# A gated residual block on one core: branch B's third stream as block products, weight sums added by transfers, and several steps reordered

## The chip, the cores and the metric

The kernel runs on one core of one Trainium2 chip. TensorE (PE in the profile) multiplies, VectorE (DVE), ScalarE (ACT) and GpSimd (POOL) do the rest, SyncE (SP) issues most transfers. The metric is the device time of one execution in microseconds (us).

## The reference

One trunk layer on 512 positions of 1024 channels, all float32. Cut to what matters here:

```python
h = rmsnorm(x, norm_mix_g)
u, v, bg, cg, xs, ga, gb = jnp.split(h @ w_in, ..., axis=-1)
a = spatial_gating(gelu(u), rmsnorm(gelu(v), norm_v_g), w_s, b_s)
c = bg * causal_dwconv(cg * xs, conv_w)
m = sigmoid(ga + b1) * (a @ w_proj_a) + sigmoid(gb + b2) * (c @ w_proj_b)
x = x + m @ w_out
z = relu(rmsnorm(x, norm_ff_g) @ w_ff1)
y = rmsnorm(x + (z * z) @ w_ff2, norm_final_g)
```

Branch B has three streams: `cg`, `xs` and `bg`, each a product of `h` with a 1024 x 1024 matrix.

## The kernel before

Everything is held transposed: channels on the 128 partitions, the 512 positions along the free dimension. Each float32 operand is split into a rounded high part (`whi`, by ScalarE, L117) and a low rest (`wlo`, by VectorE, L118), and each product is three matmuls: high x high, high x low, low x high.

Two kinds of product exist. A **unit** makes one tile of 128 output channels by 8 k-steps x 3 = 24 matmuls of 512 columns (`unit_k`, L265 to L267). A **pair** makes two tiles at once by Strassen's method in Winograd's form: seven products P1, P2, E, P6, F, P7, D, each of 4 k-steps x 3 = 12 matmuls of 256 columns (L283 to L285), 84 in all. For that the weights need sums: `s31` (two blocks, one addition of 128x1024, L218) and `s42` (two additions of 128x512, L222 and L223), so a pair splits 3.5 operands of 128x1024 where two units split 2. P1, P6, P7 and D accumulate in one half bank of PSUM, called A; E and F in another, E; P2 stands alone. Between products ScalarE copies A and E out (L300, L305, L308, L314) and VectorE adds (L301, L309, L315). P7 and D of a pair run late, inside whatever products come next (`run_late`).

Pairs are used for both gates (4 pairs each), for `cg` and `xs` (4 each) and for the first feed-forward matrix (16); units for u, `bg`, both projections, w_out and the second feed-forward matrix. Weights arrive by SyncE transfers of 1 MB into two buffers `raw`, and a list of steps (load, split, sum) is worked off a step at a time between products (`pump`), with four buffers for split operands.

The stages in order: v (0 to 51 us; 16 k-steps of 12 matmuls, bound to x and w_v coming in; its root of the mean square `rstd_of` is taken at its middle), u and mixing, gate A with projection A (to 194), four times `c_pair` (a pair for `cg`, a pair for `xs`, two units for `bg`, conv on VectorE; to 330), gate B with projection B, w_out (to 441), and four chunks of the feed-forward part (5, 4, 4 and 3 pairs, each chunk followed by units). In the first of these pairs the second `rstd_of` is taken, spread over the partitions and copied to `Rf`, which every z needs. A scheduler puts the instructions in the order in which it thinks them ready, so the order on an engine differs from the code's.

Of the kernel before, what the change touches and what calls it, by code (L numbers as in the profile page):

```python
# [36 lines left out]
def hybrid_block(ctx, tc, xT, vecs, w_v, w_main, w_pair, w_s, b_s, out_a, out_b):  # L37
# [100 lines left out]
    def load(n):  # L138
# [8 lines left out]
        else:  # L147
            nc.sync.dma_start(r, w_pair[i])
# [56 lines left out]
    sums_t = None  # L205

    def plan_pair():
# [6 lines left out]
        s31, s42 = sums_t[0].t, sums_t[1].t  # L214

        def add1():

            nc.vector.tensor_tensor(s31, raw(1, 3), raw(3, 4).broadcast_to([P, 2, S]), op=ALU.add)  # L218

        def add2():  # L220

            nc.vector.tensor_tensor(s42[:, 1, :], s31[:, 1, :], raw(1, 2)[:, 0, :], op=ALU.add)  # L222
            nc.vector.tensor_tensor(s42[:, 0, :], s42[:, 1, :], raw(0, 1)[:, 0, :], op=ALU.add)  # L223
# [3 lines left out]
        add_step(add1)  # L227
        tl["s31"] = add_operand(lambda: s31)
        add_step(add2)
        tl["s42"] = add_operand(lambda: s42)  # L230
# [58 lines left out]
    def block_pair(p, right, first, second):  # L289
# [17 lines left out]
        product(p, right, "F", E, False)  # L307
        nc.scalar.copy(c1[:, N2:], A)  # L308
# [73 lines left out]
    sums_t = slots(2, "wsum")  # L382
# [4 lines left out]
    for _ in range(KS):  # L387
        plan_pair()
        plan_pair()
        plan_units(2)  # L390
# [25 lines left out]
    def prep_v(i):  # L416
# [11 lines left out]
        nc.sync.dma_start(t, w_v[h, k])  # L428
        if i == KT + 1 or i == KT + 4:
# [6 lines left out]
        if h == 0:  # L436
            sum_squares(acc, xin[k], k)
# [27 lines left out]
    for i in range(2 * KT):  # L465
# [4 lines left out]
        if i == KT - 1:  # L470
            r = rstd_of(acc)
        vp = vparts.pop(i)
# [8 lines left out]
        if i == KT - 1:  # L481
            for b in range(NB):
                v_gelu(0, b)
        if KT <= i < KT + NB:
            v_sq(0, i - KT)
# [95 lines left out]
    for p in range(KS):  # L581
        gate(next_pair(), 0, 2 * p, sgs.__setitem__)
        if p == 0:
            for g in range(KT - LAG, KT):
                mix(g)
            give(*vt_s, *ws_s)
            ah, al = hi_lo(a_s)
# [14 lines left out]
    def c_pair(j0):  # L602
# [201 lines left out]
    wait_rf = []  # L804

    def ff1_pair(p):
# [10 lines left out]
        if p == 0:  # L817
            r2 = rstd_of(acc)
# [93 lines left out]
```

## Time and profile before

| | |
|---|---|
| time, median of 3 runs | 796.01 us (795.35 to 796.61) |
| profiled execution: time | 796.82 us |
| profiled execution: span | 795.0 us |
| TensorE busy | 786.3 us (99%) |
| VectorE busy | 567.1 us (71%) |
| ScalarE busy | 362.6 us (46%) |
| GpSimd busy | 6.3 us (1%) |
| mean granted TensorE clock | 0.996 of 2.4 GHz |

The ends of matmuls are modelled and overlap, so TensorE's 99% says that it seldom stood still, and the distance between the starts of two matmuls says how fast it went. The DMA share is the mean busy share of the core's 16 DMA engines.

### The profile page before, as it was taken

Reading aid. Unit: us, or ns where it says so; the run is one execution under the profiler, and the core shown is the slowest. Engines: PE = TensorE matmul, PEld = TensorE weight load, DVE = VectorE, ACT = ScalarE, POOL = GpSimd, SP = SyncE. Lnnn points to the kernel's source line nnn. Section 1 sums busy time; section 2 is a strip of 40 time slices with the busy share of each in tenths; the row PEclk is TensorE's granted clock in tenths of the full one; section 3 lists DMA queues with packets and bytes.
Section 4 is the critical chain, followed back from the end, with each engine's and each line's share of the span. In section 5 each row is a group of like instructions: output and inputs, shape, how many; then the busy total and the mean of one; then the engine's idle time right before and its main releaser. Section 6 shows DMA issues by size and latency. Waiting matters only on the chain.

```text
span 795.0 us, 11578 instructions
## 1 busy us (share of the span) xinstructions
PE 786.3 (99%) x4798; PEld 703.6 (88%) x4798; DVE 567.1 (71%) x854; ACT 362.6 (46%) x548; POOL 6.3 (1%) x14
## 2 busy tenths in 40 slices
PE   9999999999999999999999999999999999999996
PEld 6888899899899998988888999889988998889886
DVE  7848785556989889766679888556855687557644
ACT  8525354343344443434455566324742365226421
POOL 0000000000000000000000000000000000000000
PEclk9999999999999999999999999999999999999999
DMA  9602113321332323333633023430353025311403
GB/s 343 226 15 97 62 55 106 106 106 54 109 120 92 106 84 129 106 107 106 212 106 106 1 106 109 157 106 1 106 179 140 1 87 178 106 54 54 159 1 106
DMA packets 21444, 83.61 MB, mean 105 GB/s; under 512 B 1936, under 2 KB 2960, under 8 KB 17296
## 3 DMA queue, kind: packets, MB, share of 16 engines
q1 hardware_dynamic: 20384, 81.27, 29.3%
q10 hardware_dynamic: 1008, 1.61, 0.6%
q8 instruction: 37, 0.61, 0.3%
q14 instruction: 15, 0.12, 0.0%
HBM read 80.78 MB, written 2.10 MB: 104 GB/s over the span
## 4 chain that ended last, share of the span: by engine, by line
PE 90%; DVE 4%; DMA 3%; ACT 1%; issue 1%; POOLq 0%; DVEq 0%; ACTq 0%
PE bank L266 16%; PE bank L265 16%; PE bank L267 16%; PE bank L283 12%; PE bank L285 11%; PE bank L284 11%; PE bank L476 6%; DVE wlo L118 2%; DMA raw<-w_pair 1%; DMA raw<-w_main 1%; ACT whi L117 1%; PE bank L530 1%; DMA vec<-vecs 0%; DVE z L118 0%; DVE wsum L218 0%
## 5 line engine op out<-in xcount | busy, mean ns | idle before, releaser
L117 ACT CAST whi<-raw 128x1024 fp32r<-128x1024 f32 (+1 forms) x136 | 128.8, 950 | 185.0 <-PE bank L266 122.8
L118 DVE TENSOR_TENSOR wlo<-raw,whi 128x1024 fp32r<-128x1024 f32 (+1 forms) x136 | 148.6, 1095 | 16.7 <-ACT whi L117 14.9
L266 PE MATMUL bank<-z,whi 128*128 128x512 f32 (+1 forms) x272 | 102.7, 377 | 0.4 <-DVE z L118 0.4
L265 PE MATMUL bank<-z,whi 128*128 128x512 f32 (+1 forms) x272 | 102.8, 378 | 0.0
L267 PE MATMUL bank<-z,wlo 128*128 128x512 f32 (+1 forms) x272 | 102.4, 377 | 0.0
L117 ACT CAST whi<-wsum 128x1024 fp32r<-128x1024 f32 x64 | 67.2, 1050 | 77.0 <-PE bank L266 41.2
L118 DVE TENSOR_TENSOR wlo<-wsum,whi 128x1024 fp32r<-128x1024 f32 x64 | 78.2, 1221 | 26.6 <-ACT whi L117 26.2
L283 PE MATMUL bank<-ft,whi 128*128 128x256 f32 x256 | 73.7, 288 | 0.2
L283 PE MATMUL bank<-xc,whi 128*128 128x256 f32 x256 | 73.2, 286 | 0.2
L284 PE MATMUL bank<-ft,whi 128*128 128x256 f32 x256 | 73.0, 285 | 0.0
L285 PE MATMUL bank<-ft,wlo 128*128 128x256 f32 x256 | 72.5, 285 | 0.0
L285 PE MATMUL bank<-xc,wlo 128*128 128x256 f32 x256 | 72.4, 283 | 0.0
L284 PE MATMUL bank<-xc,whi 128*128 128x256 f32 x256 | 72.4, 283 | 0.0
L837 DVE TENSOR_TENSOR res<-bank,res 128x512 f32<-128x512 f32 x30 | 20.7, 691 | 65.5 <-PE bank L267 65.5
L266 PEld LDWEIGHTS bank<-z,whi 128*128 128x128 f32 x272 | 51.2, 188 | 9.7 <-DVE z L118 0.7
L267 PEld LDWEIGHTS bank<-z,wlo 128*128 128x128 f32 x272 | 51.2, 188 | 9.4
L265 PEld LDWEIGHTS bank<-z,whi 128*128 128x128 f32 x272 | 51.2, 188 | 9.3 <-ACT z L117 0.3
L283 PE MATMUL bank<-fb,whi 128*128 128x256 f32 x192 | 54.9, 286 | 0.0
L283 PE MATMUL bank<-x,whi 128*128 128x256 f32 x192 | 54.5, 284 | 0.0
L284 PE MATMUL bank<-fb,whi 128*128 128x256 f32 x192 | 54.4, 284 | 0.0
L285 PE MATMUL bank<-fb,wlo 128*128 128x256 f32 x192 | 54.3, 284 | 0.0
L284 PE MATMUL bank<-x,whi 128*128 128x256 f32 x192 | 54.3, 283 | 0.0
(157 smaller groups left out, 1799.6 us busy)
## 6 DMA issues: line engine op xcount, KB each, us to landing
raw<-w_main SPq DMA_DIRECT2D x36, 1024.0 KB, 5.0
raw<-w_pair SPq DMA_DIRECT2D x32, 1024.0 KB, 4.8
vraw<-w_v SPq DMA_DIRECT2D x16, 256.0 KB, 5.4
xin<-xT SPq DMA_DIRECT2D x8, 256.0 KB, 5.2
res<-xT SPq DMA_DIRECT2D x8, 256.0 KB, 4.6
out_a<-o SPq DMA_DIRECT2D x4, 256.0 KB, 2.4
wsT<-w_sT ACTq DMA_DIRECT2D x2, 256.0 KB, 4.6
bsb<-b_sb ACTq DMA_DIRECT2D x2, 256.0 KB, 5.0
```

The costliest lines, as they stand in the source:

```text
L117: nc.scalar.copy(hi, src)
L118: nc.vector.tensor_tensor(lo, src, hi.bitcast(F32), op=ALU.subtract)
L265: nc.tensor.matmul(psum, hi[:, c], act_hi[k][:, cols], start=k == 0, stop=False)
L266: nc.tensor.matmul(psum, hi[:, c], act_lo[k][:, cols], start=False, stop=False)
L267: nc.tensor.matmul(psum, lo[:, c], act_hi[k][:, cols], start=False, stop=k == KT - 1)
L283: nc.tensor.matmul(out, w_hi, x_hi, start=first and sl == 0, stop=False, skip_group_check=True)
L284: nc.tensor.matmul(out, w_hi, x_lo, start=False, stop=False, skip_group_check=True)
L285: nc.tensor.matmul(out, w_lo, x_hi, start=False, stop=sl == KS - 1, skip_group_check=True)
L476: nc.tensor.matmul(vbanks[h][b], xs[k][:, b * P : (b + 1) * P], ws, start=k == 0 and ws is vh and xs is xh, stop=k == KT - 1 and xs is xl,)
L530: nc.tensor.matmul(pm[:, b * P : (b + 1) * P], vt[b][g // 4][:, (g % 4) * P : (g % 4 + 1) * P], wsT[:, g, :], start=True, stop=True,)
L837: nc.vector.tensor_add(res[j], py, res[j])
```

## The change

Four edits:

1. `bg` becomes a third pair in each `c_pair`: its weights move from the list of units to `w_pair` (36 pairs instead of 32), and the products with `y` are taken in `b_first` and `b_second`.
2. `s31` is made by transfers: GpSimd issues a copy of two weight blocks into a buffer and a second transfer that adds the third block to both (`accum_op`). One buffer at first, three after gate A's first pair. VectorE's addition of L218 goes; `raw` gets three of the four blocks.
3. In a pair, P1, P2 and E/F have a half bank each in three banks (before: two), and the copies out of A and E stand right behind their products.
4. Steps move: v's sums of squares four k-steps later, its root from behind step 6 to behind step 7 of the first half; the copy to `Rf` behind P7 of the first feed-forward pair; in the last chunk P7 and D are no longer flushed ahead of the units, and the first two units run side by side, with their last two k-steps at the end.

```diff
-            nc.sync.dma_start(r, w_pair[i])
+            nc.sync.dma_start(r[:, :3, :], w_pair[i, :, :3, :])
...
+    s31_free, s31_of, built = [], {}, [0]
+    def build():
+        while s31_free and built[0] < w_pair.shape[0]:
+            i, s = built[0], s31_free.pop(0)
+            built[0] += 1
+            s31_of[i] = s
+            nc.gpsimd.dma_start(s.t, w_pair[i, :, 1:3, :])
+            nc.gpsimd.dma_start(s.t, w_pair[i, :, 3:4, :].broadcast_to([P, 2, S]), accum_op=ALU.add)
...
-        def add1():
-            nc.vector.tensor_tensor(s31, raw(1, 3), raw(3, 4).broadcast_to([P, 2, S]), op=ALU.add)
+        def done1():
+            s31_free.append(s31_of.pop(n))
+            build()
...
-        ba, be = bank(), bank()
-        A, P2, E = ba[:, :N2], ba[:, N2:], be[:, :N2]
+        A, P2, E = (bank()[:, :N2] for _ in range(3))
         c1, c2 = temp("c1"), temp("c2")
         product(p, right, "P1", A, True)
-        product(p, right, "P2", P2, False)
         nc.scalar.copy(c1[:, :N2], A)
+        product(p, right, "P2", P2, True)
         nc.vector.tensor_add(c1[:, :N2], P2, c1[:, :N2])
         run_late()
         product(p, right, "E", E, True)
+        nc.scalar.copy(c2[:, N2:], E)
         product(p, right, "P6", A, False)
-        nc.scalar.copy(c2[:, N2:], E)
+        nc.scalar.copy(c1[:, N2:], A)
         run_late()
         product(p, right, "F", E, False)
-        nc.scalar.copy(c1[:, N2:], A)
         nc.vector.tensor_add(c1[:, N2:], E, c1[:, N2:])
...
-        if h == 0:
-            sum_squares(acc, xin[k], k)
+        if KS <= i < KS + KT:
+            sum_squares(acc, xin[i - KS], i - KS)
...
-        if i == KT - 1:
+        if i == KT:
             r = rstd_of(acc)
+            for b in range(NB):
+                v_gelu(0, b)
...
-        pbs = []
-        for e in range(2):
-            pbs.append(bank())
-            unit_matmuls(pbs[e], xh, xl)
-        for e in range(2):
-            nc.vector.tensor_mul(ys[e], pbs[e], ys[e])
-            split_into(ch[j0 + e], cl[j0 + e], ys[e])
+        def b_first(c1):
+            nc.vector.tensor_mul(c1, c1, ys[0])
+            split_into(ch[j0], cl[j0], c1)
+        def b_second(n21, c2):
+            y = ys[1]
+            for h, src in ((0, n21), (1, c2[:, N2:])):
+                cs = slice(h * N2, (h + 1) * N2)
+                nc.vector.scalar_tensor_tensor(c2[:, cs], src, -1.0, y[:, cs], op0=ALU.mult, op1=ALU.mult)
+            split_into(ch[j0 + 1], cl[j0 + 1], c2)
+        block_pair(next_pair(), right_x, b_first, b_second)
...
-        if ck == NCH - 1:
-            flush_late()
...
+        pys = side_by_side(zh, zl) if last else {}
```

The order on the engines shows three places. GpSimd, from its last memset at the start of the program to its first power for a root (`r`; `wsum` is the buffer of `s31`), before:

```order
L71 MEMSET inv_d 128x1
L73 MEMSET expo 128x4
L352 TENSOR_TENSOR r_316<-ms_314,expo 128x4 [waits DVE_49,Pool_49]
L352 TENSOR_TENSOR r_546<-ms_544,expo 128x4 [waits DVE_49,Activation_49,Pool_49]
L352 TENSOR_TENSOR r_4197<-ms_4195,expo 128x4 [waits DVE_49,Pool_49]
```

and of the change:

```order
L71 MEMSET inv_d 128x1
L73 MEMSET expo 128x4
L213 DMA wsum_104<-w_pair 128x1024
L214 DMA wsum_104<-w_pair 128x2x512 [waits DMASW0_49]
L362 TENSOR_TENSOR r_336<-ms_334,expo 128x4 [waits DVE_49,Pool_49]
L362 TENSOR_TENSOR r_548<-ms_546,expo 128x4 [waits DVE_49,Activation_49,Pool_49]
```

The first pair's two transfers now stand at the very start, with no wait ahead of the first. Next TensorE in gate A's second pair, before, where F begins (`x4`) and P6 (`xc20`) is put in between; bank 1133 holds A and P2, bank 1134 E and F:

```order
L283 MATMUL bank_1134<-x4_113,whi_1099 128x256 [waits Activation_49]
L284 MATMUL bank_1134<-x4_113,whi_1099 128x256
L285 MATMUL bank_1134<-x4_113,wlo_1100 128x256
L283 MATMUL bank_1134<-x5_114,whi_1099 128x256
L284 MATMUL bank_1134<-x5_114,whi_1099 128x256
L283 MATMUL bank_1133<-xc20_442,whi_1099 128x256 [waits DVE_49]
L284 MATMUL bank_1133<-xc20_442,whi_1099 128x256
```

and of the change, where P6 follows E (`xc13` is E's last k-step):

```order
L294 MATMUL bank_1142<-xc13_648,whi_1074 128x256
L295 MATMUL bank_1142<-xc13_648,whi_1074 128x256
L296 MATMUL bank_1142<-xc13_648,wlo_1075 128x256
L294 MATMUL bank_1140<-xc20_444,whi_1122 128x256 [waits Activation_49]
L295 MATMUL bank_1140<-xc20_444,whi_1122 128x256
L296 MATMUL bank_1140<-xc20_444,wlo_1123 128x256 [waits DVE_49]
```

P6's first matmul waited for VectorE (the addition that reads P2 in A's bank) and now waits for ScalarE (the copy of A). Last VectorE at the end of a `c_pair`, before (`y` times the units' banks, the split of c):

```order
L218 TENSOR_TENSOR wsum_103<-raw 128x1024
L645 TENSOR_TENSOR y<-bank,y 128x512
L118 TENSOR_TENSOR wlo<-raw,whi 128x1024
L118 TENSOR_TENSOR c_1688<-y,c_1688 128x512
L301 TENSOR_TENSOR c_2321<-bank,c_2321 128x256
```

and of the change:

```order
L663 SCALAR_TENSOR_TENSOR c_1913<-bank,y 128x256
L118 TENSOR_TENSOR wlo<-raw,whi 128x512
L319 TENSOR_TENSOR c_2042<-bank,c_2042 128x256
L118 TENSOR_TENSOR c_1699<-c_1913,c_1699 128x512
```

The addition of 128x1024 is gone from VectorE, and the product with `y` is done by halves, with the pair's own additions between.

## Rows read from the trace of the kernel before

**Rows 1.** The page's first part: busy us, share of the span, instructions.
```profile
PE 786.3 (99%) x4798; PEld 703.6 (88%) x4798; DVE 567.1 (71%) x854; ACT 362.6 (46%) x548; POOL 6.3 (1%) x14
```

**Rows 2.** Timeline of PE in gate A: start us, duration us, engine, line.
```profile
112.43 0.28 PE L283 MATMUL bank<-xc,whi 128*128 128x256 f32 x1
112.54 0.28 PE L284 MATMUL bank<-xc,whi 128*128 128x256 f32 x1
...
113.86 0.40 PE L265 MATMUL bank<-a,whi 128*128 128x512 f32 x1
114.09 0.40 PE L266 MATMUL bank<-a,whi 128*128 128x512 f32 x1
```

**Rows 3.** Chain that ended last: start us, duration us, what.
```profile
5.58 19.88 PE bank L476 x84
...
205.43 0.23 PE bank L266
...
236.56 0.23 PE bank L266
```

**Rows 4.** Waits of PE's weight loads: us in total, times, longest.
```profile
PEld bank L283 <- DVE c L301: 2.8, 10, 0.6
...
PEld bank L283 <- ACT c L305: 1.4, 7, 0.2
...
PEld bank L266 <- DVE z L118: 0.7, 1, 0.7
PEld st L359 <- DVE acc L379: 0.6, 1, 0.6
```

**Rows 5.** Timeline of gate A's second pair, all engines.
```profile
128.75 0.42 DVE L301 TENSOR_TENSOR c<-bank,c 128x256 f32<-128x256 f32 x1
...
129.22 0.39 PE L283 MATMUL bank<-xc,whi 128*128 128x256 f32 x1
```

**Rows 6.** Chain at the start of the feed-forward part.
```profile
444.72 0.60 DVE acc L379
...
446.53 0.35 DVE c L301
```

**Rows 7.** Windows: from:to, length, busy us of each engine, clock, DMA share, GB/s.
```profile
205.40:236.50 31.10, 31.10 (x218) 29.16 (x217) 27.45 (x43) 13.27 (x20) 0.00 (x0) 1.00 0.28 102
```

**Rows 8.** Timeline of DVE in the first c_pair.
```profile
214.04 0.41 DVE L634 TENSOR_TENSOR z<-bank,c 128x256 f32<-128x256 f32 x1
214.38 0.68 DVE L118 TENSOR_TENSOR c<-y,c 128x512 fp32r<-128x512 f32 x1
214.98 0.48 DVE L618 TENSOR_SCALAR y<-z,vec 128x512 f32<-128x512 f32 x1
...
217.24 0.74 DVE L620 SCALAR_TENSOR_TENSOR y<-z,vec,y 128x512 f32<-128x512 f32 x1
217.90 1.22 DVE L118 TENSOR_TENSOR wlo<-wsum,whi 128x1024 fp32r<-128x1024 f32 x1
219.04 0.68 DVE L621 TENSOR_TENSOR y<-y,R 128x512 f32<-128x512 f32 x1
```

**Rows 9.** Groups by line: busy us, mean ns of one.
```profile
L352 POOL TENSOR_TENSOR r<-ms,expo 128x4 f32<-128x4 f32 (+1 forms) x5 | 5.3, 1066 | 782.5 <-DVE ms L350 782.5
```

**Rows 10.** DMA issues: KB each, median us from issue to landing.
```profile
raw<-w_pair SPq DMA_DIRECT2D x32, 1024.0 KB, 4.8
```

**Rows 11.** DMA between 17 and 21 us: queues' share of 16 engines; q1 is SyncE's, q10 ScalarE's.
```profile
q1 hardware_dynamic: 497, 1.04, 68.9%
q10 hardware_dynamic: 288, 0.52, 35.5%
```

**Rows 12.** The page's second part: DMA share in tenths, 40 slices of 19.9 us.
```profile
DMA  9602113321332323333633023430353025311403
```

**Rows 13.** Timeline of the start.
```profile
1.39 0.10 POOL L73 MEMSET expo<- 128x4 f32 x1
...
7.45 0.69 DVE L118 TENSOR_TENSOR vp<-vraw,vp 128x512 fp32r<-128x512 f32 x1
```

More of the change, by code (lines that the diff above doesn't have):

```diff
@@ L212, in raw @@
             return raw_of[ld][:, a:b, :]
-        s31, s42 = sums_t[0].t, sums_t[1].t
-        def add1():
-            nc.vector.tensor_tensor(s31, raw(1, 3), raw(3, 4).broadcast_to([P, 2, S]), op=ALU.add)
+        n = len(pairs)
+        s42 = s42_t.t
+        def done1():
+            s31_free.append(s31_of.pop(n))
+            build()
         def add2():
+            s31 = s31_of[n].t
             nc.vector.tensor_tensor(s42[:, 1, :], s31[:, 1, :], raw(1, 2)[:, 0, :], op=ALU.add)
@@ L226, in plan_pair @@
         tl["a1"] = add_operand(lambda: raw(0, 2))
-        add_step(add1)
-        tl["s31"] = add_operand(lambda: s31)
+        tl["s31"] = add_operand(lambda: s31_of[n].t)
         add_step(add2)
+        add_step(done1)
         tl["s42"] = add_operand(lambda: s42)
@@ L379, in sum_squares @@
             nc.vector.tensor_add(acc, acc, sq)
-    sums_t = slots(2, "wsum")
+    s42_t = Slot("wsum")
+    s31_free.append(Slot("wsum31"))
     plan_units(KT)
@@ L389, in hybrid_block @@
         plan_pair()
-        plan_units(2)
+        plan_pair()
     for _ in range(KS):
@@ L428, in prep_v @@
         nc.sync.dma_start(t, w_v[h, k])
+        if i == KT + 5:
+            build()
         if i == KT + 1 or i == KT + 4:
@@ L480, in hybrid_block @@
         vp.give()
[L481 to L485, printed above, removed]
+        if KT < i <= KT + NB:
+            v_sq(0, i - KT - 1)
         if i == KT + 1:
@@ L586, in hybrid_block @@
             give(*vt_s, *ws_s)
+            s31_free.extend(slots(2, "wsum31"))
+            build()
             ah, al = hi_lo(a_s)
@@ L802, in last_tiles @@
         finish_second(got["r"], hs)
-    wait_rf = []
+    wait_rf, r2 = [], []
     def ff1_pair(p):
@@ L817, in ff1_pair, with p7_and_rf, side_by_side @@
         if p == 0:
-            r2 = rstd_of(acc)
-            nc.vector.tensor_copy(Rf, spread(r2))
-            wait_rf.pop()()
+            r2.append(rstd_of(acc))
+            def p7_and_rf(p7=late.pop(0)):
+                p7()
+                nc.vector.tensor_copy(Rf, spread(r2[0]))
+                wait_rf.pop()()
+            late.insert(0, p7_and_rf)
+    def side_by_side(zh, zl):
+        pys, us = [], []
+        for e in range(2):
+            us.append(units[state["next"]])
+            state["next"] += 1
+            pump()
+            need(us[e])
+            pys.append(bank())
+            for k in range(KT - 2):
+                unit_k(pys[e], us[e], k, zh, zl)
+                if k in (0, KT // 2):
+                    run_late()
+        for e in range(2):
+            for k in (KT - 2, KT - 1):
+                unit_k(pys[e], us[e], k, zh, zl)
+            release(us[e])
+        return dict(enumerate(pys))
     done = 0
@@ L833, in hybrid_block @@
             acc2 = [acc[:, :256], acc[:, 256:]]
+        pys = side_by_side(zh, zl) if last else {}
         for j in range(KT - 2 if last else KT):
-            py = bank()
-            unit_matmuls(py, zh, zl)
+            if j in pys:
+                py = pys[j]
+            else:
+                py = bank()
+                unit_matmuls(py, zh, zl)
             nc.vector.tensor_add(res[j], py, res[j])
```

5 lines of the change are left out of this document (2 added, 3 removed).

## The prediction

> **What bounds the kernel now.** I read the page's busy shares first [rows 1]: TensorE is busy in 99% of the span, VectorE in 71%. Since matmuls overlap, I then looked at the distance of their starts [rows 2]: the twelve matmuls of 256 columns of one product take 113.86 - 112.43 = 1.43 us, 0.119 each, and two of 512 stand 0.23 apart. I use 0.120, for a little that each product's first one adds: 84 x 0.120 = 10.08 us for a pair. One `c_pair` takes 236.56 - 205.43 = 31.13 us on the chain [rows 3]; less two pairs that leaves 31.13 - 20.16 = 10.97 for its two units, or 0.2285 a matmul. So the stage holds matmuls back to back and nothing else, and TensorE's instruction stream is the bound. Third, the waits of the weight loads [rows 4]: 2.8 + 1.4 us in 17 waits at pairs' products, 0.7 ahead of the last chunk's units, 0.6 at the second root. All the standing still that could be won after the start is some 6 us of 795, so a gain can come from fewer matmul columns and from these waits, and no other engine's time counts unless it becomes the bound. The nearest to that is VectorE in `c_pair`: 27.45 of 31.10 us busy [rows 7].
>
> **The third stream on TensorE.** Four times two units (48 x 0.2285 = 10.97 us) go and a pair (10.08) comes: 4 x 0.89 = 3.5 us less. Both prices are from rows of the same stage, so the term is firm as long as TensorE stays the bound there.
>
> **What VectorE gets in that stage.** I price by the distance of starts, not by durations, since one operation starts before the last is reported ended [rows 8]: a 128x256 takes 0.34, a 128x512 0.60, a `scalar_tensor_tensor` of 512 0.66, a split or sum of 128x1024 1.14; the multiplication by a column takes at most its 0.48 and I use 0.40. Weights of a pair were 4 x 1.14 + 3 x 0.60 = 6.36 and become 5.22, because the 1.14 of L218 is gone. A `c_pair` before: two pairs' weights 12.72, two units' 2.28, six additions of a pair 2.04, `cg` 1.28, the convolutions 6.1, `bg` with its split 2.4: 26.8, against 27.45 in the window, so 2% more. After: weights 15.66, nine additions 3.06, 1.28, 6.1, 2.48: 28.6, with the 2% 29.2 us in a stage of 3 x 10.08 = 30.24. VectorE is then 97% busy and still not the bound. In bursts it falls behind: between the end of the `xs` pair and the end of the `bg` pair it has both convolutions, 12.5 us in 10.08, so about 2.4 us late. The next thing that this would stop is the third bank: seven banks turn, a pair takes three, so P2 of the pair after next takes the bank from which VectorE still has to read D. By the order that read stands some 9.5 us of VectorE's work behind the `bg` pair's beginning, and the P2 begins 10.08 + 1.44 = 11.5 us behind it: 2 us in hand. I take +0.4 us for new waits, between 0 and +3 (a wait of 0.6, the longest of [rows 4], in each of the four, and one more).
>
> **The pair's banks and copies.** Of 3.6 us that remain from 4.2 when the one long wait at the feed-forward part is set apart (the 0.6 at 446.5, where VectorE itself is late by its own chain [rows 6]), the case in [rows 5] is typical: P6 (129.22) could not start before the addition of P1 and P2 (from 128.75), because P2 lies in the bank into which P6 writes; the order shows it waiting for VectorE before and for ScalarE's copy of A after, which now stands one product earlier than the addition. E's copy, for which F waits (1.4 us), stands earlier too. I take -3.0, between -1.5 (every second wait is only replaced by one for ScalarE) and -3.6.
>
> **The other moves.** The last chunk's units no longer wait for the last z: 0.7 of waiting goes, since the last P7, D and 36 matmuls of two units (8.2 us) lie over the four operations of z's chain on at most 512 columns, 0.4 to 0.75 us each by [rows 8], 2 to 3 in all; -0.7, between 0 and -1.0. At the second root TensorE waits for VectorE's chain (acc, then two splits, then the pair's addition [rows 6]); that chain is not shorter by the change, and putting the copy to `Rf` behind P7 moves a step that no wait in [rows 4] names: 0, between 0 and -0.6. The first root now stands a k-step later, its four GELUs must free the bank that the second half's fourth product needs. Its chain is the power on GpSimd (1.07 us [rows 9]) and about as much of VectorE and ScalarE; the order puts 9 matmuls of 512 columns (2.1 us) over it: +0.2, between 0 and +1. ScalarE splits 1.5 operands more and copies four times more in each `c_pair`: even at VectorE's prices some 3.5 us where it is busy 13.27 of 31.10 [rows 7]: nothing.
>
> **The transfers.** Each pair now moves 0.79 MB by SyncE, and GpSimd 0.52 twice. In [rows 11] a megabyte and a half takes 4 us, so a pair needs about 4.7 us of the queues in 10.08; they aren't full. The sums stand three buffers ahead after gate A's first pair, some 20 us, and GpSimd waits in line only for the copy before it issues the addition; at the 4.8 us of [rows 10] for a megabyte that is well inside 10.08. Nothing, as long as an added transfer lands in the time of a plain one. At the start there is no such cover. GpSimd is free at 1.49 us [rows 13], its first copy has no wait ahead, and the queues are busy in nine tenths or more of the first slice of 19.9 us [rows 12]. When ScalarE's queue had transfers at 17 to 21 us it took 35.5% and SyncE's fell to 68.9% [rows 11]: what one queue moves, the other loses. 0.52 MB at 390 GB/s is 1.35 us, the addition as much again, or twice that if it reads its target too. The loads of the first k-step hardly meet it; the second k-step's high parts are done at 7.45 [rows 13] and needed at about 8.4 (5.58 [rows 3] + 12 x 0.23), so 1 us is in hand there, and more for each later one, since a k-step's 0.52 MB takes 1.35 us to come and 2.8 to use. I take +0.6, between 0 and +2.7 (both transfers in full).
>
> The Trainium skill, "DMA: Bandwidth & Descriptors", Issuing engines are not separate DMA queues, says that transfers from several engines run on the same 16 DMA engines and interleave, so that issuing elsewhere saves only issue time. By that rule the two early transfers cost the start up to their full 2.7 us; if GpSimd's had a way of their own the start would cost nothing; the 68.9% bears the rule out.
>
> **Sum.** -3.5 + 0.4 - 3.0 - 0.7 + 0 + 0.2 + 0.6 = -6.0 us. From the profiled execution's 796.8 that gives 790.8; the median of the runs shown is 0.8 lower, 796.0, and my forecast is against it: **790.0 us**. Its own range is 788 to 792.5.
>
> **Rivals.** *The waits only move*: with VectorE at 97% and copies in line on ScalarE the pairs keep their 4 us of waits, and the third stream's gain and the z wait come alone: 796.0 - 3.5 - 0.7 + 0.8 + 0.4 = 793.0. For it speaks that there is so little room; against, the order, in which the named waits are gone. *No change* (794.4 to 797.6; 0.2%, 1.6 us, is about what a measurement of this kernel can tell): the start costs its 2.7 and the waits stay.
>
> *VectorE becomes the bound by GpSimd's issuing* (the other side). No run here shows GpSimd issuing a transfer. If each of the six in a `c_pair` stopped VectorE for as long as GpSimd's one measured operation (1.07 us [rows 9]), the stage would be 29.2 + 6.4 = 35.6 us, 4.5 over the 31.1 of now, four times 18; with the other gains 796.0 + 18 - 2.9 = 811. It decides from (30.24 - 29.2) / 6 = 0.17 us each on; the third stream has lost its gain at 0.32, and slower than now by 0.2% the kernel is from about 0.5 (7.6 us over 24 transfers more). In the other stages VectorE has room. The page "SBUF — State Buffer", Who interferes with whom, of the Trainium skill, says that GpSimd shares a pair of ports with VectorE, held by one of them for a whole instruction, though two-source operations on VectorE are stopped only by GpSimd's reads; by that rule this rival's price would be near nothing, since nearly all of VectorE's work here has two sources.
>
> *The sums come late*: in the 13 pairs in a row (`c_pair` and gate B's first) each microsecond by which GpSimd's round exceeds 10.08 adds up, less the 20 in hand; it decides at 11.6 us a round, more than twice the 4.8 of a megabyte. At 15 us it would be 13 x 4.9 - 20 = 44 us there, 834 in all.
>
> **Chances.** Forecast 0.56; better than 788 (all waits gone, no cost at the start) 0.07; the waits only move 0.18; no change 0.08; VectorE bound 0.06; sums late 0.05. The range 787.5 to 794.5 holds the first three. Faster by over 0.2% is 0.81, within 0.08, slower 0.11.
>
> **What would show it.** The `c_pair`s' distance on the chain: 30.2 to 30.6 us if the first term holds, 32 or more if VectorE binds. PE's waits on the additions at pairs' products: gone, or with ScalarE's name. The first matmul at 5.6 us and the v stage's end at 51: later by what the early transfers cost. VectorE's operations in `c_pair` longer than in [rows 8]: the port. A weight load that waits for `wsum`: sums late. I would be wrong above all if an adding transfer takes several times a plain one, or if the stage without slack falls out of step by more than the 2 us in hand.

## The result and the profile after

The kernel got slower: 807.7 us, median of four executions (804.2 to 811.1), against 795.9 for the kernel before on the same chip; ratio 1.0147, 95% interval 1.0102 to 1.0193. The profiled execution took 804.2 us, the shortest of the four, so the profile shows 7.3 us of loss against the profile before, and not the 11.8 of the medians. In two kernels below that differ from this one only in the v stage's code, profiled at 806.1 and 808.0 us, branch B and the feed-forward part together take 2.7 and 4.8 us longer than here: that is where the executions differ. One execution of the second of these kernels took 1557.3 us and is in no number below. First the page of the kernel after, to be held against [rows 1]: busy time, and the DMA queues, where q0 is GpSimd's, which was not there before, and q1 SyncE's.

```profile
PE 782.3 (98%) x4942; PEld 708.3 (88%) x4942; DVE 547.1 (68%) x854; ACT 373.4 (47%) x572; POOL 69.7 (9%) x86
...
q1 hardware_dynamic: 19872, 71.83, 25.7%
q0 software_dynamic: 14976, 37.75, 20.9%
```

TensorE has 4 us less to do and VectorE 20, and the span is 7.4 us longer. Where that is, the starts of matmuls tell (timeline of PE, us). The v stage goes from its first matmul to the first of the units, branch A from there to the last matmul of its projection, branch B from there to the last of its own, and the feed-forward part from its first matmul to the program's last; the output projection ahead of it takes 43.75 in both.

| | v stage | units and branch A | branch B | feed-forward |
|---|---|---|---|---|
| before | 45.96 | 135.44 | 209.83 | 347.72 |
| after | 55.22 | 135.37 | 210.61 | 344.77 |

So the v stage lost 9.3 us; branch B, where 3.5 were to be won, lost 0.8; the feed-forward part won 3.0.

**The v stage.** `wsT` holds the mixing weights, which ScalarE's queue loads in two halves. Timeline of the kernel after: DMA issues of SyncE and ScalarE, then VectorE and TensorE (start, duration, and in brackets the idle time ahead and what ended it).

```profile
20.05 0.38 SPq L144 DMA_DIRECT2D raw<-w_main  x1
...
20.83 0.34 ACTq L502 DMA_DIRECT2D wsT<-w_sT  x1
...
28.50 1.28 SPq L439 DMA_DIRECT2D vraw<-w_v  x3
...
29.53 0.48 DVE L505 MEMSET wsT<- 64x512 f32 x1 [5.75 <-DMA wsT<-w_sT]
...
37.69 7.50 PE L491 MATMUL bank<-vp,x 128*128 128x512 f32 x19 [5.27 <-ACT vt L454]
```

VectorE zeroes a corner of wsT and stands 5.75 us until that load has landed. The kernel before, in the same place:

```profile
21.41 0.48 DVE L493 MEMSET wsT<- 64x512 f32 x1 [0.87 <-DMA wsT<-w_sT]
```

Behind the memset in its queue lie six operations, and then the first root. Chain of the kernel after in the same place:

```profile
33.07 2.27 DVE wlo L118 x2
35.34 0.08 DVE ms L360
...
35.57 1.36 POOL r L362
...
36.95 0.70 ACT vt L454
...
37.69 7.50 PE bank L491 x19
```

Root, power, GELU, and only then the bank that TensorE has been waiting for since 32.4. After that the matmuls are slow. Windows of the kernel after (from:to, length, busy us of each engine, granted clock, DMA share, GB/s):

```profile
37.60:43.40 5.80, 5.71 (x13) 4.46 (x14) 5.80 (x18) 4.81 (x9) 0.00 (x0) 0.50 0.15 61
43.40:60.80 17.40, 17.40 (x81) 14.50 (x80) 5.03 (x10) 3.66 (x7) 0.00 (x0) 0.99 0.18 62
```

From 37.1 to 43.9 us the clock is at 0.50, the lower of its two levels (1.2 GHz). In the 5.8 us shown there are 13 matmuls: 5.80 - 13 x 0.2285 = 2.8 us more than at the higher level. The stop of 5.3 and these 2.8 make 8.1 of the 9.3; 0.8 more are two waits for ScalarE's splits of v (at 8.6 us the longer).

**Branch B.** Waits of PE's weight loads in the kernel after, 281 to 407 us (total, times, longest). From 196 to 281 us there is none.

```profile
PEld bank L294 <- ACT c L324: 3.0, 3, 1.4
PEld bank L294 <- ACT c L314: 2.5, 2, 2.2
```

The waits for VectorE's additions [rows 4] are gone, as forecast, and in their place stand longer ones for ScalarE's copies. The chain through one of them:

```profile
307.18 0.60 DVE wlo L118
...
307.81 5.15 DMA raw<-w_pair
...
313.06 0.42 ACT whi L117
...
314.00 0.38 ACT c L324
```

The copy of P7 (L324) is short, and its product was long done (the last matmul of P7 began at 310.0 us). It is behind the cast of the next pair's weights (L117) in ScalarE's queue, the cast waits for the load, and the load was issued when VectorE had split the last block, a22, of the pair that held raw's buffer. The split of a22, which product D alone uses, has one buffer, so it has to wait for D of the pair before. This is the loop through raw's buffer: D, the split of a22, the next load, its landing, the casts, and the products that lead to the next D.

### The profile page after: what moved, and what is told of

Read it like the earlier page. It is cut to its first block, busy times and chain, and to the rows that moved or that the text cites. A ratio compares the mean times of both kernels' runs of the same rounds, so it can differ in the third digit from the quotient of the medians.

```text
span 802.4 us, 12035 instructions
## 1 busy us (share of the span) xinstructions
PE 782.3 (98%) x4942; PEld 708.3 (88%) x4942; DVE 547.1 (68%) x854; ACT 373.4 (47%) x572; POOL 69.7 (9%) x86
## 4 chain that ended last, share of the span: by engine, by line
PE 71%; DMA 13%; DVE 10%; issue 3%; ACT 3%; POOL 0%; SPq 0%; DVEq 0%; POOLq 0%; ACTq 0%
PE bank L276 14%; PE bank L277 14%; PE bank L278 14%; PE bank L294 8%; PE bank L295 8%; PE bank L296 8%; DMA raw<-w_pair 7%; PE bank L491 5%; DVE wlo L118 5%; DMA raw<-w_main 4%; ACT whi L117 2%; DMA vraw<-w_v 1%; DMA wsum<-w_pair 1%; DVE wsum L234 1%; DVE wsum L233 1%
## 5 line engine op out<-in xcount | busy, mean ns | idle before, releaser
L117 ACT CAST whi<-raw 128x1024 fp32r<-128x1024 f32 (+1 forms) x136 | 126.5, 937 | 191.5 <-PE bank L277 112.8
L118 DVE TENSOR_TENSOR wlo<-raw,whi 128x1024 fp32r<-128x1024 f32 (+1 forms) x136 | 146.1, 1079 | 21.2 <-ACT whi L117 20.5
L117 ACT CAST whi<-wsum 128x1024 fp32r<-128x1024 f32 x72 | 75.5, 1050 | 81.1 <-PE bank L277 42.0
L118 DVE TENSOR_TENSOR wlo<-wsum,whi 128x1024 fp32r<-128x1024 f32 x72 | 88.0, 1222 | 19.4 <-ACT whi L117 18.6
L294 PE MATMUL bank<-xc,whi 128*128 128x256 f32 x320 | 90.9, 284 | 2.2 <-ACT c L324 2.2
L295 PE MATMUL bank<-xc,whi 128*128 128x256 f32 x320 | 90.7, 283 | 0.0
L296 PE MATMUL bank<-xc,wlo 128*128 128x256 f32 x320 | 90.7, 283 | 0.0
L294 PE MATMUL bank<-x,whi 128*128 128x256 f32 x240 | 68.4, 285 | 2.5 <-ACT c L314 2.5
L296 PE MATMUL bank<-x,wlo 128*128 128x256 f32 x240 | 68.0, 283 | 0.0
L295 PE MATMUL bank<-x,whi 128*128 128x256 f32 x240 | 68.0, 283 | 0.0
L294 PEld LDWEIGHTS bank<-xc,whi 128*128 128x128 f32 x320 | 61.5, 192 | 3.6 <-ACT c L324 3.0
L295 PEld LDWEIGHTS bank<-xc,whi 128*128 128x128 f32 x320 | 61.5, 192 | 0.6
L296 PEld LDWEIGHTS bank<-xc,wlo 128*128 128x128 f32 x320 | 61.5, 192 | 0.0
L276 PEld LDWEIGHTS bank<-z,whi 128*128 128x128 f32 x272 | 51.3, 189 | 9.0
```

The source lines that it names most:

```text
L117: nc.scalar.copy(hi, src)
L118: nc.vector.tensor_tensor(lo, src, hi.bitcast(F32), op=ALU.subtract)
L276: nc.tensor.matmul(psum, hi[:, c], act_hi[k][:, cols], start=k == 0, stop=False)
L294: nc.tensor.matmul(out, w_hi, x_hi, start=first and sl == 0, stop=False, skip_group_check=True)
L295: nc.tensor.matmul(out, w_hi, x_lo, start=False, stop=False, skip_group_check=True)
L296: nc.tensor.matmul(out, w_lo, x_hi, start=False, stop=sl == KS - 1, skip_group_check=True)
```

## The experiments

Times are medians, ratios are against the kernel before on the same chip. The stages, as above, are those of one profiled execution each, which for the first sum held took 801.2 us and for copies and banks only 795.1.

| run | us | ratio, 95% | v | A | B | ff |
|---|---|---|---|---|---|---|
| after | 807.7 | 1.0147 (1.010 to 1.019) | 55.2 | 135.4 | 210.6 | 344.8 |
| v order put back | 805.3 | 1.0139 (1.011 to 1.017) | 54.3 | 135.2 | 213.4 | 346.9 |
| first sum's code moved | 805.1 | 1.0126 (1.010 to 1.015) | 54.5 | 135.5 | 211.3 | 346.8 |
| first sum held | 798.7 | 1.0050 (1.003 to 1.007) | 45.7 | 135.3 | 213.1 | 349.0 |
| memset late | 802.1 | 1.0078 (1.006 to 1.009) | 49.0 | 135.4 | 210.8 | 348.7 |
| second transfer plain | 804.8 | 1.0116 (1.010 to 1.014) | 55.4 | 134.7 | 210.5 | 346.2 |
| sums on VectorE | 792.2 | 0.9962 (0.995 to 0.998) | 45.4 | 134.7 | 212.1 | 342.0 |
| third stream only | 798.8 | 1.0047 (1.003 to 1.006) | 45.9 | 135.4 | 213.1 | 346.5 |
| transfers in B only | 791.5 | 0.9951 (0.994 to 0.997) | 45.4 | 134.7 | 210.2 | 342.2 |
| units, no transfers | 788.7 | 0.9917 (0.990 to 0.993) | 45.7 | 134.7 | 208.5 | 342.1 |
| copies and banks only | 789.7 | 0.9921 (0.991 to 0.994) | 50.3 | 134.7 | 208.5 | 343.7 |
| two a22, transfers in B | 785.6 | 0.9873 (0.986 to 0.989) | 45.4 | 134.9 | 205.0 | 342.0 |
| six temporaries | 791.9 | 0.9946 (0.993 to 0.996) | 45.4 | 134.9 | 212.1 | 342.1 |
| two a22, sums on VectorE | 787.8 | 0.9896 (0.988 to 0.991) | 45.5 | 134.9 | 207.3 | 342.0 |
| two a22, transfers in all | 786.3 | 0.9878 (0.986 to 0.990) | 45.8 | 135.5 | 205.0 | 342.0 |

### The v stage

**The order of the v stage put back.**

```diff
-        if KS <= i < KS + KT:
-            sum_squares(acc, xin[i - KS], i - KS)
+        if h == 0:
+            sum_squares(acc, xin[k], k)
...
-        if i == KT:
+        if i == KT - 1:
             r = rstd_of(acc)
```

> The kernel after, with the order of the v stage put back (squares beside each k-step's split, root, roots' GELUs and squares of v a k-step earlier as before); the early GpSimd transfers of the first sum stay. The profile after has the v stage 9.3 us longer: TensorE waits 5.4 us at 32.0 us for a bank that the GELU frees, behind it VectorE's memset of wsT had waited 5.75 us for its load, and then matmuls stand 0.43 us apart for some 6 us (about 3 us more). Theory 1 (it takes both: the early transfers make the load of wsT late, and the later root stands behind the memset on VectorE): here the root is taken before the memset, the 5.4 us and the slow matmuls go, and the start of u comes at 52 to 53 us instead of 60.8; against before 1.002 to 1.007, some 799 us. Theory 2 (the transfers alone cost it, by taking the queues' time): u still begins at 58 to 61 us, ratio 1.012 or more. Theory 3 (the later root alone): u at 51.5, as before, ratio about 1.002.

Its stages in the table are those of another execution, of 808.0 us:

> The same kernel as the one with the order of the v stage put back, for a profile, since that of the first run fell into a disturbed execution; its three other times were 805.0 to 808.7. By these times u should begin at 59 to 61 us here too (the transfers alone are enough); if it begins at 52 to 54 the loss of that kernel lies elsewhere.

1.0139 and a v stage of 54.3 us: theory 2. With the old order, too, VectorE's queue has the memset (30.58) ahead of the first root (34.05), and TensorE stands 5.8 us for the GELU. The later root is not what costs the 9.3 us.

**The first sum late**, twice.

```diff
         if i == KT + 5:
-            build()
...
+    build()
     Rp = spread(r)
```

> The kernel after, with the order of the v stage as changed, but the first sum's two GpSimd transfers issued only behind the v stage. Theory 1 (both are needed): the load of wsT lands at about 22 to 25 us as before, the memset holds VectorE 1 us or so, u begins at 51.5 to 53 us, ratio 1.002 to 1.006, some 798.5 us. Theory 2 (the early transfers alone): u at 51 to 51.5 us, as before. Theory 3 (the later root alone, whose chain hangs behind the memset whenever wsT lands): u at 57 to 61 us and a ratio of 1.01 or more.

This told nothing apart: GpSimd's queue has no earlier work that must come first, and it still issued the copy at 1.56 us. It is the kernel after once more, and so are its times. Then with a write that the transfer must wait for:

```diff
+    nc.vector.tensor_copy(s31_free[0].t[:, 0, :NB], rv)
+    build()
```

> The kernel after, with the first sum's two transfers really held back: VectorE writes four columns of the second root into their target ahead of them, so that GpSimd issues them behind the second root's power, at some 50 us, half way through the unit stage in which the queues are mostly idle; the earlier attempt only moved the code, and GpSimd still issued them at 1.6 us. Theory 1 (the early transfers cost the v stage all of its 9.3 us): u begins at 50.5 to 51.5 us, all else as in the kernel after, so 797 to 798.5 us, ratio 1.001 to 1.004. Theory 2 (only a part is theirs, the later root or GpSimd's queue has the rest): u at 54 us or later, ratio above 1.006.

Theory 1 as to the start: the v stage takes 45.7 us, less than before. Timeline of this kernel, in the order of the issues:

```profile
16.07 0.34 ACTq L500 DMA_DIRECT2D wsT<-w_sT  x1
...
17.35 0.43 SPq L144 DMA_DIRECT2D raw<-w_main  x1
20.58 1.28 SPq L439 DMA_DIRECT2D vraw<-w_v  x3
...
21.54 0.48 DVE L503 MEMSET wsT<- 64x512 f32 x1 [0.62 <-DMA wsT<-w_sT]
```

Without the early transfers wsT's load goes out 1.3 us ahead of the megabyte for raw and lands at 21.3; with them it goes out 0.8 us behind it and lands at 29.3 (the memset starts 0.2 us behind the landing in both). The load of wsT stands in ScalarE's queue behind its work on x: the last load of x landed at 18.7 us instead of 13.9, 4.8 later, and wsT's load went out 4.8 later. And SyncE's last three loads for v go out when wsT lands, from 20.58 here and from 28.50 in the kernel after: the program has the first and the last of them wait on the semaphores that wsT's two halves signal (in the kernel after these landed at 28.48 and 29.30, and the two loads went out at 28.50 and 29.35).

The whole kernel is a little above what was expected (798.7 for 797 to 798.5). In the profiles branch B and the feed-forward part are 6.7 us longer here than in the kernel after, by waits for ScalarE's copies (10.6 us in 11; there 6.2 in 10), but these profiles are of executions of 801.2 us (median 798.7) and 804.2 (median 807.7). Against the kernel before, the medians are 3.4 and 11.8 us more, 8.5 apart, where the v stage is 9.5 shorter: about 1 us is left for the other stages.

**The memset behind the v stage**, with the early transfers.

```diff
-            nc.vector.memset(wsT[64:128, :, 0:64], 0.0)
...
+    nc.vector.tensor_scalar(zero, vsum[:, 1, 0:1], 0.0, None, op0=ALU.mult)
+    tri = wsT[64:128, :, 0:64]
+    nc.vector.tensor_scalar(tri, tri, zero[64:128, :], None, op0=ALU.mult)
```

> The kernel after, early transfers and all, except that VectorE zeroes the corner of wsT only behind the v stage (by a multiplication with a zero that is made from the last sum of squares). In the kernel after, wsT's load is issued by ScalarE at 20.83 us, 0.8 behind a megabyte for raw (20.05), and lands at 29.5; with the first sum held it is issued at 16.07, 1.3 ahead of raw (17.35), and lands at 21.5. Theory 1 (the start's lateness flips these two loads; VectorE, with the first root behind its memset in line, then stands 5.75 us, the GELUs are late and the clock falls): with the memset out of the way the wait of 5.4 us at 32 us and the slow matmuls from 38 us go, and only the late first k-steps are left: u at 52 to 54.5 us instead of 60.8, 799 to 801.5 us in all, ratio 1.005 to 1.008. Theory 2 (the root is late by itself, by the loads for v): u still at 58 to 61 us, ratio 1.011 or more.

Theory 1: u begins at 54.5 us, 6.3 sooner. The chain of this kernel at wsT's load:

```profile
20.86 7.37 DMA wsT<-w_sT
...
28.25 3.19 DMA vraw<-w_v
```

and its window behind that:

```profile
31.80:54.50 22.70, 20.72 (x97) 16.93 (x95) 12.36 (x31) 10.81 (x19) 1.04 (x1) 1.00 0.29 98
```

What is left, 3.3 us more than with the sum held, is the loads for v behind wsT's; TensorE stands 2.0 us for a GELU, and the clock stays at 1.00.

**The second transfer plain instead of adding.**

```diff
-.broadcast_to([P, 2, S]), accum_op=ALU.add)
+.broadcast_to([P, 2, S]))
```

> The kernel after, with GpSimd's second transfer of each sum as a plain one of the same shape that overwrites instead of adding; the addition of the blocks is left out, all else is the same. In the profile after GpSimd's queue took 167.7 us of the 16 engines (20.9% of 802.4) for 36 plain transfers and 36 adding ones, SyncE's 206 us for 71.83 MB, 2.87 us a megabyte; if the 36 plain ones of 0.52 MB cost that rate, 1.50 us each, an adding one costs 3.15, twice as much. Theory 1 (the start is short of the queues' time, and an adding transfer takes twice a plain one): the queue's time falls to about 108 us, u begins at 56 to 59 us instead of 60.8, the waits behind ScalarE's copies in branch B get shorter by a third, in all 1 to 4 us less than the kernel after. Theory 2 (what counts is that GpSimd issues transfers at all, not the adding): u at 60 to 61 us, ratio 1.012 to 1.015. Theory 3 (the adding is all of it): u at 52 us or less, under 797 us.

The queues, to be held against the page of the kernel after:

```profile
q1 hardware_dynamic: 19872, 71.83, 25.8%
q0 software_dynamic: 10368, 37.75, 14.3%
```

This kernel leaves out the addition. 14.3% of 803.9 us is 115 us for 72 plain transfers, 1.60 each. The adding made it 167.7: (167.7 - 115) / 36 = 1.46 more, 3.06 for an adding one, 1.9 times a plain one. And it changed nothing: v stage 55.4, branch B 210.5. Theory 2: it is enough that the transfers come at that time, 1 MB of them.

### Branch B

**All sums on VectorE; the third stream alone.**

```diff
-            nc.sync.dma_start(r[:, :3, :], w_pair[i, :, :3, :])
+            nc.sync.dma_start(r, w_pair[i])
...
+        def add1():
+            nc.vector.tensor_tensor(s31_t.t, raw(1, 3), raw(3, 4).broadcast_to([P, 2, S]), op=ALU.add)
```

> The kernel after, with the first weight sum of each pair back on VectorE and all four blocks of a pair loaded by SyncE, so that GpSimd issues no transfer at all; third stream, copies, banks, roots and squares stay as changed. In the profile after the stretch of 12 pairs in a row lost 0.8 us where the forecast had won 3.5, in waits of 0.3 to 2.1 us (5.6 in all) for ScalarE's copies, which stand behind splits of weights whose load had just been issued. Theory 1 (the added transfers' load on the queues makes these loads late): the waits go as far as VectorE lets them; by the distances of starts VectorE then has 29.2 + 3 x 1.14 x 1.02 = 32.7 us of work against 30.24 of TensorE, so a stage of 32.7 instead of 31.1, 4 x 1.6 = 6.4 us worse than before in that stretch, by another bound; the v stage as in the run with the first sum late. In all 1.005 to 1.012. Theory 4 (the loads are late since three pairs in a row use one raw buffer after another, whoever adds): the waits named ScalarE's copies stay and VectorE's come on top, ratio 1.01 or more. If the split of the pair's work on VectorE is not the bound even so, the stretch comes out 2 to 4 us shorter than before and the ratio is under 1.0.

```diff
-        plan_units(2)
+        plan_pair()
...
+        block_pair(next_pair(), right_x, b_first, b_second)
```

> The kernel before with one part of the change alone: the third stream as a pair, with the sums on VectorE, and copies, banks, v stage and last chunk as before. TensorE's work shrinks by 4 x 0.89 = 3.5 us. Theory A (VectorE has room): 792.5 us, ratio 0.9955. Theory B (VectorE binds: 26.8 - 6.36 to 3 x 6.36 of weights, three more additions, 31.8 us or with 2% 32.5 against 30.24 of TensorE): a stage of 32.5 against 31.1 now, 4 x 1.4 = 5.6 us longer, 801.5 us, ratio 1.007. Between them, if waits at pairs' products eat the gain: 0.998 to 1.002.

With everything else of the change, but no transfers, the kernel is faster than before, by 0.4%: both theories missed that, since they left out that the v stage and the feed-forward part give 6.2 us. Branch B takes 212.1, 2.2 more than before, where 6.4 more had been expected; waits named ScalarE's cast of weights stand there (3.7 us in 5). The third stream alone, in the kernel before, costs 3.2 us in branch B, between theory B and none. So without transfers the pair of the third stream loses, and the transfers take off only 1.5.

**Transfers in branch B alone; no third stream, no transfers.**

```diff
-        while s31_free and built[0] < w_pair.shape[0]:
+        while s31_free and built[0] < HI:
...
+        if not gp:
+            add_step(add1)
```

> The kernel after, with sums by transfers only for the 16 pairs of branch B (three streams and its gate); for branch A's gate and the feed-forward part VectorE adds and SyncE loads all four blocks. With all sums on VectorE the v stage ended 10 us sooner than in the kernel after, the stages of branch A's gate 0.7 and the feed-forward part 2.8, branch B 1.5 us later. Theory 1 (the transfers cost time where the queues or ScalarE are short, and help a little where VectorE is short): the sum of the better parts, 792.2 - 1.5 = 790.7 us, ratio 0.994. Theory 2 (branch B with transfers is late since the stages before it run ahead differently): as with all sums on VectorE, 792 to 793. A profit of the full forecast, 790.0 less the 0.6 of the start, would be here if the third stream alone had been mis-sized by nothing: 789.4.

> The kernel before with the copies, P2's bank, root and squares and the last chunk's changes, but the third stream as units and no transfers by GpSimd. Theory 1 (the third stream as pairs, with 97% or more of VectorE asked for, costs more than TensorE's 3.5 us, as the third stream alone did with 1.0047): branch B at 207 to 209.8 us instead of 212.1, the feed-forward part 3.5 to 4 us shorter than before, in all 787.5 to 790 us, ratio 0.990 to 0.9935, the fastest. Theory 2 (the copies and banks made the room that the third stream needs, and it gains with them): 793 to 795.5 us, ratio 0.997 to 1.0.

The first lies between its two theories by its time (791.5; 790.7, and 792 to 793), and is theory 1 by branch B's 210.2. The second is theory 1, and 2.9 us faster than the first: up to here the best version was one without the third stream's pairs and without transfers.

**A second buffer for a22.**

```diff
-    a22_busy = [False]
+    w22free = [0, 1]
...
+        tl["a22"] = add_operand(lambda: raw(2, 3), n=1)
+        add_step(lambda: load(ld + 2))
         tl["s42"] = add_operand(lambda: s42)
-        tl["a22"] = add_operand(lambda: raw(2, 3), n=1)
-        add_step(lambda: load(ld + 2))
```

> The kernel with transfers in branch B only (791.54 us; branch B 210.2 us), with a second buffer for the split of a22, which then needn't wait for D of the pair before; a22 is split ahead of s42, and raw's buffer is given back and loaded again some 8 us sooner. Room for it comes from two of the eight temporaries. Theory 1 (what holds TensorE in the 12 pairs in a row is the loop through raw's buffer: D, then the split of a22 on a VectorE that is late, then a load of 5.3 us, then a1's split, with ScalarE's copies in line behind it): the waits for ScalarE's copies go, branch B takes 206 to 208 us, in all 787 to 789.5, ratio 0.990 to 0.993. Theory 2 (VectorE's 97% is the bound, and the loads are late only because it is): branch B stays at 209.5 us or more, with VectorE's or ScalarE's name at the waits, ratio 0.9945 or more. If six temporaries are too few, slower than that.

Better than theory 1's range: 785.6 us, branch B 205.0. All of PE's waits in this kernel:

```profile
PE st L78 <- DVE warm L65: 1.0, 1, 1.0
PE bank L502 <- ACT vp L117: 0.2, 1, 0.2
```

and its window in branch B:

```profile
200.00:310.00 110.00, 110.00 (x919) 110.00 (x918) 104.15 (x176) 60.74 (x94) 19.45 (x22) 1.00 0.69 183
```

TensorE has no gap in 110 us, with VectorE busy in 95% and GpSimd issuing as before. The loads for pairs even take longer (median 5.8 us in 196 to 316, 5.3 in the kernel after); they are only issued sooner. The loop through raw's buffer can be read from these issues: in the kernel after SyncE's loads for pairs go out 10.5 us apart (mean of nine, 213.7 to 307.8 us), more than the 10.08 that TensorE needs for a pair, and here 10.1 apart (203.4 to 294.1). With that the third stream's pairs gain 208.48 - 205.04 = 3.4 us over units, the forecast's first term; neither kernel has a wait of TensorE there.

Three controls:

> The kernel with transfers in branch B only (791.54 us), with six temporaries instead of eight and one buffer for a22 as before. If the second buffer of a22 made the gain of 5.9 us: 791.5 us or a little more. If fewer temporaries made it (by holding the engines' order differently): 786 us.

> The kernel after with the second buffer for a22 and six temporaries, but all sums on VectorE and no transfers by GpSimd. Theory 1 (VectorE is the next bound: by the forecast's distances 32.7 us of work in a stage of 30.24): branch B takes 205.0 + 4 x 2.5 = 215 us, less what stands in reserve at its beginning, 211 to 215; in all 791.5 to 795.5 us. Theory 2 (only the loop through raw's buffer held the stage, and the transfers are of no use): branch B 205 to 207, 785.5 to 787.5 us.

> The kernel after with the second buffer for a22 and six temporaries, the first sum's transfers held back behind the second root, and sums by transfers for all 36 pairs. Theory 1 (the 0.7 us that branch A's gate and the 2.8 that the feed-forward part lose with transfers are the same loop: raw's buffer given back late and a load that lands late): they go as well, 785.5 to 787 us, as with transfers in branch B only. Theory 2 (it is the queues' load by itself): 788 to 790 us.

Six temporaries alone give 791.9: the gain is the buffer's (with its earlier load), not theirs. With the sums on VectorE branch B takes 207.3, between the theories and nearer the second; in the window

```profile
200.00:310.00 110.00, 109.19 (x910) 108.99 (x909) 109.03 (x179) 56.38 (x91) 0.00 (x0) 1.00 0.28 97
```

VectorE is busy in 99% and TensorE no longer all the time, so it is the next bound, but it costs 2.3 us and not 6 or more; that branch B's gate, with room on VectorE, takes up what is late would fit and was not tried. The transfers are thus worth 2.1 us, once the loop through raw's buffer is gone. With transfers for all pairs and the first held back, the feed-forward part is as short as without: theory 1, it was the same loop there. In branch A it is not: 135.5 us with transfers and 134.9 without, as before the second buffer.

### The copies and banks

```diff
-        ba, be = bank(), bank()
-        A, P2, E = ba[:, :N2], ba[:, N2:], be[:, :N2]
+        A, P2, E = (bank()[:, :N2] for _ in range(3))
```

and the copies a product earlier, in the kernel before.

> The kernel before with one part of the change alone: the copies earlier and a bank of its own for P2. The forecast had -3.0 us for it, between -1.5 and -3.6: 792.4 us, ratio 0.9955 to 0.998. The kernel with everything but the third stream and the transfers is 6.7 us faster than before, of which the last chunk's units and the v stage should have 1.1. Theory 1 (the copies and banks are the rest): 789.8 us, ratio 0.993. Theory 2 (the forecast's term, and the last chunk and the second root have 3 us): 792.4.

789.7, 6.0 us less than before: theory 1, twice the forecast's term. The one wait of this kind left among PE's weight loads:

```profile
PEld bank L283 <- ACT c L313: 0.2, 1, 0.2
```

Its profiled execution is the slowest of five (795.1, the others 789.1 to 789.9), because of its v stage: there VectorE stood 5.3 us ahead of the same memset until the second half of wsT had landed (issued at 17.1 us, together with raw's megabyte, 9.3 us to the landing), TensorE 3.0 for the GELU, and the clock fell to 0.50 for 3.4 us. So the start is on the edge without transfers, too; they pushed it over in every profile that has them early.

How far the forecast's rows account for the 6.0 can be seen from the starts. The distances of the 2,784 starts at 256 columns sum to 340.7 us before and 334.9 here, 5.8 less. But one stretch of the kernel before, in the first feed-forward pair behind the second root, is not a wait (window of the kernel before; the third number from the end is the granted clock):

```profile
447.03:450.44 3.41, 3.41 (x17) 3.41 (x18) 2.51 (x5) 0.53 (x2) 1.91 (x1) 0.50 0.02 5
```

The clock is at 0.50, and matmuls of 256 columns stand 0.21 us apart instead of 0.12: about 1.5 us. With the copies and banks alone it is at 1.00 there. This leaves 4.3 us for the stops themselves, close to the 4.2 of [rows 4]. The medians differ by 6.0 all the same, although most executions of the kernel before show a mean granted clock of 0.998 (the profiled one 0.996) and so seem not to have this stretch; where the rest of the 6.0 lies is open.

## Why the prediction was wrong

Forecast 790.0, measured 807.7. Compared profile with profile (790.8 and 804.2), 13.4 us are missing: 8.5 in the v stage (+9.3 for +0.8), 4.6 in the other three (-2.2 for -6.8), and the rest behind the last matmul. The medians miss 4.3 more, which this profile cannot show.

**The step that failed most is the early transfers' price**, "+0.6, between 0 and +2.7 (both transfers in full)". It took the queues' time as the most that they can cost. The order of issues was overlooked: raw's megabyte was issued 2.7 us later than with the sum held and wsT's load 4.8, which put it behind raw's (x's last load had landed 4.8 us later, too), and on wsT's landing hang VectorE's memset with the first root behind it, and SyncE's last loads for v. The v stage paid 9.3, over three times the upper end. The adding transfer took 1.9 times a plain one; the prediction names this case ("or twice that if it reads its target too"), but its upper end counts two plain ones. With the measured 1.60 + 3.06 it would have been 4.7, still half of what was paid, and the adding had no part in it, as the run with a plain second transfer shows. The rule of the Trainium skill that was weighed there, that transfers issued by several engines interleave on the same 16 DMA engines ("DMA: Bandwidth & Descriptors", Issuing engines are not separate DMA queues), has the direction right, as the held sum shows (45.7 us for 55.2). The 2.7 us worked out from it are the transfers' own time, and too little.

**The first root a k-step later**, +0.2, between 0 and +1: it cost nothing. With the sum held or on VectorE the v stage has the later root and takes 45.4 to 45.8 us, 0.2 to 0.6 less than before.

**The third stream**, -3.5: the size is right (3.4 with the second buffer), its condition, "as long as TensorE stays the bound there", failed. **The step "+0.4 us for new waits, between 0 and +3", failed with it**: it looked for the next wait at the third bank and found 2 us in hand. TensorE never waited there. The place was raw's buffer: a22 can't be split before D of the pair before is done, VectorE comes to the split late, the load is issued then and takes 5 us. In 12 pairs in a row this loop takes 10.5 us a pair instead of 10.08. Pairs loaded ahead hide that for 85 us in this execution (for 55 to 66 in four others), and then TensorE stops five times. The new waits cost 5.6 us (210.6 in branch B for 205.0 with the second buffer). That the loop had slack when units stood between the pairs is read from the rows without such waits, and was not tried by itself. "Nothing" for the transfers in this stage was meant for wsum, and holds there: no weight load waits for it. In the feed-forward part, however, the transfers cost 2.8 us by the same loop (344.8 for 342.0), and some 7 in the profiles with the sum held and the memset late.

**VectorE at 97% and not the bound**: right, by the 95% of the window without a gap. With the sums on it, it binds, though more mildly than the same sum says.

**Copies and banks**, -3.0, between -1.5 and -3.6: right in the mechanism, too small in size; alone they gave 6.0. The prediction took 3.0 of the 4.2 us of [rows 4], and by the distances the stops gave 4.3. Another 1.5 in the profiled execution were the clock behind the second root, for which the prediction has no term. The rest is open.

**The last chunk**, -0.7, was not tried by itself; the wait for z's split [rows 4] is gone. With the other moves, without transfers and with units, the feed-forward part takes 342.1 us, and with the copies and banks alone 343.7. The last chunk and the second root, forecast at -0.7 and 0, thus gave 1.6 together; the waits for z and at the second root [rows 4] are gone.

**The rivals.** "VectorE bound by GpSimd's issuing" gave 811 and was near the result by chance: a `wlo` of 128x1024 takes 1.22 us in branch B after as before [rows 8], and the second buffer closed all gaps with GpSimd issuing 19.45 us of 110. The sign that was named for it, longer operations on VectorE, did show, in the multiplications by a column: of the eight in branch B of the kernel after, two took 0.58 and 0.74 us instead of 0.48 [rows 8], both while GpSimd issued a transfer. That is 0.4 us in all. "The sums come late" was not seen. "The waits only move" was half right: they moved to ScalarE's copies, and grew (4.2 us of weight loads' waits before, 9.2 after).

## What to carry to other kernels

Before work is added to a stage whose queues are full, write down the order of the issues and what hangs on each landing; a load that goes out a microsecond too late can land 8 us later, as wsT's did here, and what waits behind it, here a memset and a root, can cost the clock as well. When pairs follow each other without a pause, follow each buffer round (last reader, next load, landing, first use), and not only the engines' sums: a second buffer for a quarter of a pair's weights was worth 5.9 us here. Before a gain is put down to stalls, look at the granted clock in the stretch, before and after: 1.5 us of what the copies and banks gave by the distances was the clock.

## What was not expected of the hardware

An adding transfer of 0.52 MB took the queues 3.06 us and a plain one 1.60, and still neither the v stage nor branch B cared which it was. The clock was at 0.50 for 6.8 us after TensorE had stood 5.3 us in the kernel after, and for 3.4 us after it had stood 3.0 in the run with copies and banks alone. After stops of 2.0 us it was 1.00 in the run with the late memset, and 0.50 for 3.4 us (320.1 to 323.5) in branch B of the run with the first sum held. It was at 0.50 for 3.4 us in branch B with the v order put back, too (330.0 to 333.4), where no stop was longer than 1.7 us, and in the kernel before behind the second root, where TensorE had stood 0.4 us and worked on eight matmuls of one column. What decides between these was not tried.
